# New source order at both ends of the FFN, with only TensorE held to the source from the output projection on

## The chip, the cores and the metric

The kernel runs on one core of one Trainium2 chip. Its time is what the device takes for one launch, in microseconds (us). Five engines work side by side, each through its own queue of instructions and in the order of that queue: TensorE (PE in the rows; PEld is its loading of weights), VectorE (DVE), ScalarE (ACT), GpSimd (POOL) and SyncE (SP), which issues nearly all transfers from memory. They wait for each other through semaphores.

## The reference, cut to what matters

One step of a one-layer encoder: two branches of attention, mixed into `m`, then an output projection, an FFN and a final norm. What the change touches is the last part:

```python
def _merge_ffn(h, ya, yb, ga, gb, w_out, norm_ffn, w_up, w_down):
    m = jax.nn.sigmoid(ga) * ya + jax.nn.sigmoid(gb) * yb
    h = h + jnp.einsum('btd,de->bte', m, w_out)
    u = jnp.einsum('btd,df->btf', _rmsnorm(h, norm_ffn), w_up)
    return h + jnp.einsum('btf,fd->btd', jnp.square(jax.nn.relu(u)), w_down)
...
    y_prompt = _rmsnorm(h_p[:, N_META:], norm_final)
    y_sample = _rmsnorm(h_s, norm_final)
```

The model width D is 1024, the FFN width 4096, and the kernel treats 544 tokens at once (512 of the prompt and 32 of the sample stream).

## The kernel before, in words

**Arithmetic.** All large products are made in a short float format with a correction: a matrix `a` is split into a high part (`split_hi`, a copy by ScalarE, line 121) and a low part (`split_lo`, a subtraction by VectorE, line 124), and a product is the sum of three matmuls, high by high, low by high and high by low (`mm`, line 118). So every weight that arrives from memory costs one ScalarE and one VectorE instruction before TensorE can use it, and so does every operand.

**Output projection.** The loop near line 1272 runs over the eight 128-row blocks of D in the order 0, 4, 1, 5, 2, 6, 3, 7 (`WO_ORDER`). For each it takes the split weights `wh`/`wl`, makes 48 matmuls into two parts of PSUM (288 and 256 tokens), adds the result to `xres` on VectorE (line 1283), and calls `operands(d)`. That function builds the operands of the FFN's up products out of two `xres` blocks: the tiles `ba`, `bb`, `b2`, and their splits `hh0` to `hh3` and `hl0` to `hl3`, of which number 3 is last, since it needs `xres3` and `xres7`.

**FFN up.** 16 steps, `up_pair(g)` for g = 0 to 15, each 256 columns of w_up. A step uses a scheme with seven products in place of eight: X with weights a11, V with s1, X again with s2, V with s4, X with s3, Y with a12, X with a22; each is 12 matmuls of 272 columns. Between the products ScalarE copies X or V out of PSUM (`fa`, `fb`, lines 1376, 1390, 1393, 1403, 1417), and the copy of the first X into `fa` must be done before the third product may add onto X. The weights of a step are made by `pair_prep(g)`, a generator: each `go(prep, n)` puts n more of its steps into the program (loads `wr1`, `wr2`; the sums `s31` and `s24` on VectorE, lines 297 to 308; then the splits, whose high parts are called `whi`, `s2h` and so on, their low parts `wlo`, `s2l`). It runs one step ahead. Two buffers of `whi`/`wlo` and three of raw weights are shared by all.

**FFN down.** The result of a step, squared, is split into `uh`/`ul`. The 16 steps form eight chunks: step 0, then pairs of steps, then steps 13 to 15. The down product of a chunk is eight calls `down(i)`, put between the products of the next chunk's first two steps, at the places n = 1, 3, 5, 6 of each. Its weights `dr` are loaded two calls ahead and split one call ahead (`dh`/`dl`). The last chunk's down product has no step left to lie between: it is the tail. There `last(d, a, b, ..)` does the eight blocks d for the first 288 tokens, then for the other 256; `last_evac` scales (`dt`, line 1523) and adds; `final_part` transposes finished blocks by TensorE into `ps_fin`, from which ScalarE takes squares (`fj`, line 1328) and VectorE writes `ytok` (line 1329); `final_norm` scales and stores.

**What sets the order.** Up to the output projection a scheduler places the instructions of all engines. From line 1205 on, `manual_schedule` holds TensorE, ScalarE and VectorE to the order of the source; the loads on SP go by the scheduler.

Of the kernel before, what the change touches and what calls it, by code (L numbers as in the profile page):

```python
# [15 lines left out]
P = 128  # L16
# [31 lines left out]
def tile_hybrid_step(  # L48
# [182 lines left out]
    def add_unit(key, parts):  # L231
        units.append((key, parts))

    def unit_prep(n):
        key, parts = units[n]
        raw = wpool.tile([P, KD, P], F32, tag="raw", name=f"wr_{n}", bufs=3)
        k = 0
        for src in parts:
            kk = src.shape[0] // P
            SP.dma_start(raw[:, k: k + kk, :], src.rearrange("(k p) n -> p k n", p=P))  # L240
            k += kk
        if parts[0].shape[0] == D and key[0] in IN_KEYS:
# [20 lines left out]
    def pair_prep(g):  # L263
# [45 lines left out]
        split(A, 1, ["s1"], s31[:, 1:2])  # L309
        yield  # L310
        if g == 0:
            for i, nm in enumerate(("s2", "s4")):
                split(one(nm), 0, [nm], s24[:, i: i + 1])
        else:
            B = t(wpool, "whi", bufs=2), t(wpool, "wlo", bufs=2)
            split(B, 0, ["s2", "s4"], s24)
# [862 lines left out]
    for d in range(KD):  # L1179
# [23 lines left out]


    ordered = ctx.enter_context(tc.manual_schedule(
        engines={mybir.EngineType.PE, mybir.EngineType.Activation, mybir.EngineType.DVE}))


    act_set = ACT.preload_act_table_set("natural_log_exp_and_others")
# [62 lines left out]
    for n, d in enumerate(WO_ORDER):  # L1272
        xr = tmp([TM], f"xres{d}")
        POOL.tensor_tensor(xr, xh[:, d, M0:].bitcast(F32), xl[:, d, M0:].bitcast(F32), ALU.add)
        wh, wl = use(("wo", d))
        if n == KD - 2:
            prep = pair_prep(0)
            go(prep, 3)
        if n == KD - 1:
            go(prep, 4)  # L1280

        def evac_o(ci, a, b, ps, xr=xr):
            DVE.tensor_tensor(xr[:, a:b], ps, xr[:, a:b], ALU.add)
# [81 lines left out]
    def up_pair(g):  # L1365
# [13 lines left out]
        if g == 0:  # L1379

            own, prep = prep, pair_prep(1)
            go(prep, 1)
            drain(own)
        else:
            drain(prep)
            prep = pair_prep(g + 1) if g < 15 else iter(())
            go(prep, 1)
        yield
        product(V, W["s1"], BM, True)
        ACT.activation(fb[:, 1, :], vv, AF.Copy)  # L1390
# [49 lines left out]

    def down(i):
        c, d = dn[i]
        if i + 1 < len(dn):
            go(dpreps[i + 1], 1)
        dstart(i + 2)
        wh, wl = downs.pop((c, d))
# [40 lines left out]
            DVE.reciprocal(r2[:, a:b], r2[:, a:b])  # L1487


    dstart(0)  # L1490
    dstart(1)
    for c in range(NCH):
        for jj, g in enumerate(CHUNKS[c]):
            for n, _ in enumerate(up_pair(g)):
                if c == 0 and n == 5:
                    go(dpreps[0], 1)
                if c > 0 and jj < 2 and n in (1, 3, 5, 6):
                    d = 4 * jj + (1, 3, 5, 6).index(n)
                    down(8 * (c - 1) + d)
                    if c == 1:  # L1500
                        square(d)
                    if c == 2 and d == 2:
                        norm2()
    while tail:
        tail.pop(0)()
    alloc_ytok()
# [1 line left out]

    c = NCH - 1

    def last(d, a, b, psf):
        wh, wl = downs[c, d]
        ps = psf(f"ps_dn{c}_{d}_{a}")
        K = 2 * len(CHUNKS[c])
        for k in range(K):
# [3 lines left out]
        return ps  # L1519

    def last_evac(d, a, b, ps):
        dt_ = fpool.tile([P, TM], F32, tag="dt", name=f"dt{c}_{d}_{a}", bufs=2)
# [5 lines left out]
    (a, b), T0, T1 = OC[0], range(3), range(3, NTT)  # L1528
    for d in range(KD):
        if d + 1 < KD:  # L1530
            go(dpreps[8 * c + d + 1], 1)
        dstart(8 * c + d + 2)
        ps = last(d, a, b, (psa, pss)[d % 2])
        if d == 4:
            final_part(0, T0)
        rest_a = last_evac(d, a, b, ps)
    a, b = OC[1]
    for d in range(KD):
        ps = last(d, a, b, (psa, pss)[d % 2])
        if d == 0:  # L1540
            final_part(1, T0)
        if d == 1:
# [4 lines left out]
        if d == 7:
            final_part(1, T1)
            final_early(3, NTT)
        rest = last_evac(d, a, b, ps)  # L1550
# [36 lines left out]
```

## Time and profile before

| | us |
|---|---|
| median of the runs (3) | 843.84 |
| the runs, lowest to highest | 840.65 to 845.9 |
| the profiled execution, its own time | 841.46 |
| its span, first to last instruction | 839.7 |
| TensorE busy within the span | 804.4 (96%) |
| VectorE busy | 585.3 (70%) |
| ScalarE busy | 366.2 (44%) |
| GpSimd busy | 123.3 (15%) |

Moments below are us from the start of that span. The output projection takes it from 392.8 to 444.05, the FFN's steps with the downs between them from 444.3 to 783.7, the tail the rest. Reading the profile: a line of an instruction gives its start, its duration, its engine and line, and in brackets how long the engine had been idle before it and whose instruction released it. Matmuls overlap: each is listed with 0.28 to 0.30 us, but the next starts 0.12 to 0.13 us later, and this distance is what one costs.

### The profile page before, as it was taken

Reading aid. Unit: us, or ns where it says so; the run is one execution under the profiler, and the core shown is the slowest. Engines: PE = TensorE matmul, PEld = TensorE weight load, DVE = VectorE, ACT = ScalarE, POOL = GpSimd, SP = SyncE. Lnnn points to the kernel's source line nnn. Section 1 sums busy time; section 2 is a strip of 40 time slices with the busy share of each in tenths; the row PEclk is TensorE's granted clock in tenths of the full one; section 3 lists DMA queues with packets and bytes.
Section 4 is the critical chain, followed back from the end, with each engine's and each line's share of the span. In section 5 each row is a group of like instructions: output and inputs, shape, how many; then the busy total and the mean of one; then the engine's idle time right before and its main releaser. Section 6 shows DMA issues by size and latency. Waiting matters only on the chain.

```text
span 839.7 us, 15161 instructions
## 1 busy us (share of the span) xinstructions
PE 804.4 (96%) x6093; PEld 772.6 (92%) x6093; DVE 585.3 (70%) x1139; ACT 366.2 (44%) x722; POOL 123.3 (15%) x132
## 2 busy tenths in 40 slices
PE   8998999999999999999997999999999999999995
PEld 6867898898999989999997999999999999999995
DVE  5856358798768554466667888776667777798764
ACT  5761454555446523232445673343433344333332
POOL 4305112221121493025000000000000000000000
PEclk8999999999999999999998999999999999999998
DMA  8513223422521132323123142323333333322402
GB/s 244 153 47 100 51 48 98 122 77 59 143 64 51 52 100 77 96 82 101 55 84 115 48 126 73 111 81 90 90 102 101 101 92 98 101 77 63 113 2 107
DMA packets 133813, 75.38 MB, mean 90 GB/s; under 512 B 15056, under 2 KB 129024, under 8 KB 133744
## 3 DMA queue, kind: packets, MB, share of 16 engines
q1 hardware_dynamic: 132704, 72.27, 30.4%
q0 software_dynamic: 1024, 2.14, 1.1%
q8 instruction: 48, 0.79, 0.4%
q14 instruction: 21, 0.17, 0.1%
q10 hardware_dynamic: 16, 0.00, 0.0%
HBM read 69.57 MB, written 4.83 MB: 89 GB/s over the span
## 4 chain that ended last, share of the span: by engine, by line
PE 72%; DVE 13%; ACT 5%; POOL 3%; issue 3%; DMA 3%; SPq 0%; ACTq 0%; POOLq 0%; DVEq 0%
PE ps_dn L118 22%; PE ps_x L118 11%; PE ps_v L118 6%; PE ps_gb L118 5%; PE ps_ga L118 5%; PE ps_fv L118 3%; PE ps_y L118 3%; PE ps_yb L118 2%; PE ps_ya L118 2%; PE ps_wo L118 2%; PE ps_fk L118 2%; DVE wl L124 2%; ACT wh L121 1%; DMA wr<-in_w_in_dram 1%; PE ps_s L118 1%
## 5 line engine op out<-in xcount | busy, mean ns | idle before, releaser
L118 PE MATMUL ps_dn<-uh,dl 128*128 128x288 f32 (+1 forms) x416 | 120.7, 290 | 0.0
L118 PE MATMUL ps_dn<-uh,dh 128*128 128x288 f32 (+1 forms) x416 | 119.7, 288 | 0.9 <-ACT uh L121 0.9
L118 PE MATMUL ps_dn<-ul,dh 128*128 128x288 f32 (+1 forms) x416 | 120.1, 289 | 0.2 <-DVE ul L124 0.2
L121 ACT ACTIVATE wh<-wr 128x1024 fp32r<-128x1024 f32 x46 | 48.5, 1055 | 87.9 <-PE ps_yb L118 24.3
L124 DVE TENSOR_TENSOR wl<-wr,wh 128x1024 fp32r<-128x1024 f32 x46 | 68.7, 1494 | 19.2 <-ACT wh L121 18.8
L118 PEld LDWEIGHTS ps_dn<-uh,dh 128*128 128x128 f32 x416 | 78.5, 189 | 1.1 <-ACT uh L121 1.1
L243 POOL TENSOR_TENSOR wr<-wr,gmix 128x1024 f32<-128x1024 f32 x30 | 58.0, 1937 | 143.2 <-DMA wr<-in_w_in_dram 104.5
L118 PEld LDWEIGHTS ps_dn<-uh,dl 128*128 128x128 f32 x416 | 78.3, 188 | 0.5 <-DVE dl L124 0.5
L118 PEld LDWEIGHTS ps_dn<-ul,dh 128*128 128x128 f32 x416 | 78.3, 188 | 0.5 <-DVE ul L124 0.5
L1468 DVE TENSOR_TENSOR acc<-ps_dn,acc 128x288 f32<-128x288 f32 x96 | 41.1, 438 | 30.4 <-PE ps_dn L118 30.4
L1307 POOL DMA_DIRECT2D gfin<-in_norm_final_dram x1 | 0.6, 607 | 374.1 <-DVE s3l L124 374.1
L118 PE MATMUL ps_x<-hh,whi 128*128 128x272 f32 x124 | 36.1, 291 | 1.5 <-ACT fa L1376 1.3
L124 DVE TENSOR_TENSOR dl<-dr,dh 128x512 fp32r<-128x512 f32 (+1 forms) x56 | 36.3, 648 | 1.7 <-ACT dh L121 1.6
L118 PE MATMUL ps_x<-hh,wlo 128*128 128x272 f32 x124 | 35.9, 290 | 0.5 <-DVE wlo L124 0.5
L118 PE MATMUL ps_v<-hl,whi 128*128 128x272 f32 x124 | 36.0, 290 | 0.0
L118 PE MATMUL ps_v<-hh,whi 128*128 128x272 f32 x124 | 35.8, 289 | 0.0
L118 PE MATMUL ps_x<-hl,whi 128*128 128x272 f32 x124 | 35.8, 289 | 0.0
L118 PE MATMUL ps_v<-hh,wlo 128*128 128x272 f32 x124 | 35.8, 288 | 0.0
L124 DVE TENSOR_TENSOR wlo<-s,whi 128x512 fp32r<-128x512 f32 (+1 forms) x31 | 29.4, 947 | 6.3 <-ACT whi L121 6.3
L935 ACT ACTIVATE sb<-sb,m 128x144 f32<-128x144 f32 (+3 forms) x32 | 18.3, 573 | 35.1 <-DVE m L930 35.1
L121 ACT ACTIVATE dh<-dr 128x512 fp32r<-128x512 f32 (+1 forms) x56 | 33.2, 593 | 0.0
L1403 ACT ACTIVATE x<-ps_x 128x272 f32<-128x272 f32 x16 | 6.4, 397 | 53.2 <-PE ps_x L118 53.1
(511 smaller groups left out, 2467.0 us busy)
## 6 DMA issues: line engine op xcount, KB each, us to landing
wr<-in_w_up_dram SPq DMA_DIRECT2D x62, 256.0 KB, 3.4
wr<-in_w_in_dram SPq DMA_DIRECT2D x30, 512.0 KB, 3.9
dr<-in_w_down_dram SPq DMA_DIRECT2D x48, 256.0 KB, 3.1
wr<-in_w_out_dram SPq DMA_DIRECT2D x8, 512.0 KB, 3.9
dr<-in_w_down_dram SPq DMA_DIRECT2D x8, 384.0 KB, 3.9
cb<-cPd SPq DMA_DIRECT2D x8, 264.0 KB, 4.1
x_t<-in_x_prompt_dram SPq DMA_DIRECT2D x4, 512.0 KB, 5.7
gvraw<-in_w_in_dram SPq DMA_DIRECT2D x4, 512.0 KB, 8.6
```

The source lines that it names most:

```text
L118: return TE.matmul(out, lhsT, rhs, start=start, stop=stop, skip_group_check=True)
L121: ACT.activation(out, in_, AF.Copy)
L124: (eng or DVE).tensor_tensor(out, in_, hi.bitcast(F32), ALU.subtract)
L243: POOL.tensor_tensor(raw, raw, gmix.unsqueeze(2).to_broadcast([P, KD, P]), ALU.mult)
L935: exps.append(ACT.activation(sb, sb, AF.Exp, bias=m, scale=-1.0, accum_out=rs).ins)
L1307: POOL.dma_start(late["gfin"], norm_final.partition_broadcast(P))
L1403: ACT.activation(x3, xv, AF.Copy)
L1468: DVE.tensor_tensor(acc[d][:, a:b], ps[:, :w], acc[d][:, a:b], ALU.add)
```

## The change

Apart from the order, nothing is computed differently; both programs have the same number of instructions on each engine. There are six edits:

- **Scheduler.** `manual_schedule` keeps TensorE alone; ScalarE and VectorE are ordered by the scheduler to the end of the program.
- **First step's weights.** The loads of `pair_prep(0)` are put into the source one output block earlier; of its steps, one comes at the third block from the end, two at the second and three at the last, where it was three and four; the rest is spread over the first three products of step 0. A last load of output weights is issued ahead of them (`unit_load`).
- **First downs.** For chunk 0 the table `EARLY` starts the eight calls `down` at n = 3 of step 1 (three in step 1, five in step 2), no longer at n = 1.
- **Norm.** `norm2`, two matmuls and four VectorE instructions, comes one chunk later.
- **Last chunk's weights.** They are prepared at n = 2 and 4 of step 15, no longer by `down`.
- **Tail.** The first two blocks start with the parts of the chunk that are long done (steps 13 and 14: `range(K - 2)`), and take those of step 15 only after both; weights are prepared three blocks ahead; the three tiles of `final_part(0, T0)` come one by one after d = 4, 5 and 6; the last block of the second half is cut in two, with `final_part(1, T1)` in the middle.

```diff
     ordered = ctx.enter_context(tc.manual_schedule(
-        engines={mybir.EngineType.PE, mybir.EngineType.Activation, mybir.EngineType.DVE}))
+        engines={mybir.EngineType.PE}))
...
+        if n == KD - 3:
+            unit_load(nxt[0])
+            prep = pair_prep(0)
+            go(prep, 1)
         if n == KD - 2:
-            prep = pair_prep(0)
+            go(prep, 2)
+        if n == KD - 1:
             go(prep, 3)
-        if n == KD - 1:
-            go(prep, 4)
...
             own, prep = prep, pair_prep(1)
             go(prep, 1)
-            drain(own)
+            go(own, 1)
...
         product(V, W["s1"], BM, True)
         ACT.activation(fb[:, 1, :], vv, AF.Copy)
+        if g == 0:
+            go(own, 1)
         yield
         product(X, W["s2"], BN, False)
         ACT.activation(fa[:, 1, :], xv, AF.Copy)
+        if g == 0:
+            drain(own)
...
-        if i + 1 < len(dn):
+        if i + 1 < 8 * (NCH - 1):
             go(dpreps[i + 1], 1)
...
+    REGULAR = [{1: (0,), 3: (1,), 5: (2,), 6: (3,)}, {1: (4,), 3: (5,), 5: (6,), 6: (7,)}]
+    EARLY = [{3: (0,), 5: (1,), 6: (2,)}, {1: (3,), 2: (4,), 3: (5,), 5: (6,), 6: (7,)}]
...
-                if c > 0 and jj < 2 and n in (1, 3, 5, 6):
-                    d = 4 * jj + (1, 3, 5, 6).index(n)
+                for d in (EARLY if c == 1 else REGULAR)[jj].get(n, ()) if 0 < c and jj < 2 else ():
                     down(8 * (c - 1) + d)
                     if c == 1:
                         square(d)
-                    if c == 2 and d == 2:
+                    if c == 3 and d == 2:
                         norm2()
+                if jj == 2 and n in (2, 4):
+                    go(dpreps[8 * c + n // 2 - 1], 1)
+                    dstart(8 * c + n // 2 + 1)
...
+    first = [last_ps(d, 0) for d in range(2)]
+    for d in range(2):
+        last(d, 0, first[d], range(K - 2))
+    prep_last(2)
     for d in range(KD):
...
+        if d < 2:
+            ps = first[d]
+            last(d, 0, ps, range(K - 2, K))
+        else:
+            ps = last_ps(d, 0)
+            last(d, 0, ps, range(K))
+        rest_a = last_evac(d, 0, ps)
+        prep_last(d + 3)
+        if 4 <= d < 7:
+            final_part(0, [d - 4])
     for d in range(KD):
-        ps = last(d, a, b, (psa, pss)[d % 2])
+        ps = last_ps(d, 1)
+        if d < KD - 1:
+            last(d, 1, ps, range(K))
+        else:
+            last(d, 1, ps, range(3))
+            final_part(1, T1)
+            last(d, 1, ps, range(3, K))
+            final_early(3, NTT)
```

The order of instructions shows at three places what the diff alone doesn't.

**VectorE, from the end of the output projection into step 0, before.** `xres7` is the sum of the last output block, from which the last operands are built (`bb3`, `b23`, `hl3`); `wlo_0`, `s2l_0`, `s4l_0`, `s3l_0` are low parts of the weights of step 0.

```order
L124 TENSOR_TENSOR hl3_4675<-ba3_5161,hh3_4671 128x544
L124 TENSOR_TENSOR wlo_0_5171<-wr1_0_5098,whi_0_5170 128x512
L124 TENSOR_TENSOR wlo_0_5171<-s31_0_5104,whi_0_5170 128x512
L124 TENSOR_TENSOR s2l_0_5177<-s24_0_5106,s2h_0_5176 128x512
L124 TENSOR_TENSOR s4l_0_5181<-s24_0_5106,s4h_0_5180 128x512
L124 TENSOR_TENSOR s3l_0_5185<-s31_0_5104,s3h_0_5184 128x512
L1283 TENSOR_TENSOR xres7_5168<-ps_wo7_0_5188,xres7_5168 128x288
L1283 TENSOR_TENSOR xres7_5168<-ps_wo7_1_5214,xres7_5168 128x256
L1253 SCALAR_TENSOR_TENSOR bb3_5162<-ba3_5161,b23_5240 128x272
L1254 TENSOR_TENSOR bb3_5162<-b23_5240,bb3_5162 128x272
L124 TENSOR_TENSOR hl3_4675<-bb3_5162,hh3_4671 128x544
```

The same place with the change; `dl0_0` is the low part of the first weights of the down product, whose transfer is `dr0_0`, and `s31_1` belongs to the weights of step 1.

```order
L1294 TENSOR_TENSOR xres7_5168<-ps_wo7_0_5180,xres7_5168 128x288
L124 TENSOR_TENSOR dl0_0_5389<-dr0_0_5253,dh0_0_5388 128x256
L124 TENSOR_TENSOR s4l_0_5289<-s24_0_5106,s4h_0_5288 128x512
L1294 TENSOR_TENSOR xres7_5168<-ps_wo7_1_5206,xres7_5168 128x256
L124 TENSOR_TENSOR s3l_0_5306<-s31_0_5104,s3h_0_5305 128x512
L124 TENSOR_TENSOR wlo_1_5347<-wr1_1_5281,whi_1_5346 128x512
L1261 SCALAR_TENSOR_TENSOR bb3_5162<-ba3_5161,b23_5232 128x272
L1262 TENSOR_TENSOR bb3_5162<-b23_5232,bb3_5162 128x272
L124 TENSOR_TENSOR hl3_4675<-b23_5232,hh3_4671 128x544
L1269 SCALAR_TENSOR_TENSOR ba3_5161<-bb3_5162,b23_5232 128x272
L304 TENSOR_TENSOR s31_1_5330<-wr1_1_5281,wr2a_1_5282 128x1024
L124 TENSOR_TENSOR hl3_4675<-bb3_5162,hh3_4671 128x544
```

The second half of `xres7` stood behind the low parts of all five weights, and stands behind two instructions now, of which one needs the transfer `dr0_0`; the `hl3` that is made of `bb3`, on which the third product waits, has `s31_1` ahead of it.

**ScalarE, same place, before.** `fa0` is the copy of the first X of step 0, on which the third product waits.

```order
L121 ACTIVATE hh3_4671<-ba3_5161 128x544
L121 ACTIVATE whi_0_5170<-wr1_0_5098 128x512
L121 ACTIVATE whi_0_5170<-s31_0_5104 128x512
L121 ACTIVATE s2h_0_5176<-s24_0_5106 128x512
L121 ACTIVATE s4h_0_5180<-s24_0_5106 128x512
L121 ACTIVATE s3h_0_5184<-s31_0_5104 128x512
L1252 ACTIVATE b23_5240<-xres7_5168,prmT_187 128x544
L121 ACTIVATE hh3_4671<-bb3_5162 128x544
L1376 ACTIVATE fa0_5267<-ps_x0_5269 128x272
```

And with the change:

```order
L121 ACTIVATE hh3_4671<-ba3_5161 128x544
L121 ACTIVATE dh0_0_5388<-dr0_0_5253 128x256
L121 ACTIVATE s4h_0_5288<-s24_0_5106 128x512
L121 ACTIVATE dh0_1_5494<-dr0_1_5255 128x256
L121 ACTIVATE s3h_0_5305<-s31_0_5104 128x512
L121 ACTIVATE whi_1_5346<-wr1_1_5281 128x512
L1260 ACTIVATE b23_5232<-xres7_5168,prmT_187 128x544
L1387 ACTIVATE fa0_5259<-ps_x0_5261 128x272
L121 ACTIVATE hh3_4671<-b23_5232 128x544
```

The splits of a11, s1 and s2 have moved away ahead of `hh3`, `fa0` no longer stands behind a split of `bb3`, and two splits of weights of the down product, `dh0_0` and `dh0_1`, stand in front of it.

**ScalarE at the start of step 15, before.** `whi7_0` is the high part of the first weights of the tail, which takes a buffer that TensorE must have left; `fa15` is the copy on which the third product of step 15 waits.

```order
L121 ACTIVATE uh14_8949<-fa14_8951 128x544
L1417 ACTIVATE fb14_8952<-ps_x14_8953 128x272
L121 ACTIVATE whi7_0_9202<-dr7_0_9144 128x768
L1376 ACTIVATE fa15_9242<-ps_x15_9244 128x272
L121 ACTIVATE uh14_8949<-fb14_8952 128x544
L121 ACTIVATE a22h_15_9261<-wr1_15_8974 128x512
```

With the change:

```order
L121 ACTIVATE uh14_8949<-fa14_8951 128x544
L1432 ACTIVATE fb14_8952<-ps_x14_8953 128x272
L121 ACTIVATE a22h_15_9257<-wr1_15_8974 128x512
L121 ACTIVATE uh14_8949<-fb14_8952 128x544
L1387 ACTIVATE fa15_9238<-ps_x15_9240 128x272
L1401 ACTIVATE fb15_9239<-ps_v15_9241 128x272
L121 ACTIVATE whi7_0_9287<-dr7_0_9144 128x768
```

`whi7_0` has moved behind the copies `fa15` and `fb15`.

## Rows read from the trace of the kernel before

**Rows 1.** The page: TensorE's busy time; its granted clock in 40 slices, in tenths.

```profile
PE 804.4 (96%) x6093; PEld 772.6 (92%) x6093; DVE 585.3 (70%) x1139; ACT 366.2 (44%) x722; POOL 123.3 (15%) x132
...
PEclk8999999999999999999998999999999999999998
```

**Rows 2.** Busy time by stretch: its length, PE, PEld, DVE, ACT, POOL, granted clock, DMA.

```profile
444.00:451.00 7.00, 3.62 (x26) 3.14 (x25) 5.46 (x11) 4.22 (x9) 0.00 (x0) 1.00 0.38 111
451.00:458.20 7.20, 6.33 (x28) 6.00 (x29) 6.17 (x11) 3.67 (x8) 0.00 (x0) 0.54 0.41 120
...
500.00:770.00 270.00, 269.45 (x2135) 268.91 (x2134) 207.07 (x360) 105.25 (x202) 0.00 (x0) 1.00 0.32 91
770.00:783.60 13.60, 12.34 (x99) 12.11 (x98) 10.17 (x20) 3.28 (x7) 0.61 (x1) 1.00 0.46 127
```

**Rows 3.** TensorE in time, output projection to step 3: start, duration, [idle before <- releaser].

```profile
400.07 1.08 PE L118 MATMUL ps_wo<-mh,wh 128*128 128x288 f32 x7
...
406.13 1.08 PE L118 MATMUL ps_wo<-mh,wh 128*128 128x288 f32 x7
...
444.31 0.39 PE L118 MATMUL ps_x<-hh,whi 128*128 128x272 f32 x1 [0.27 <-ACT whi L121]
...
450.98 0.40 PE L118 MATMUL ps_x<-hh,s2h 128*128 128x272 f32 x1 [2.67 <-ACT fa L1376]
...
454.81 0.43 PE L118 MATMUL ps_v<-hh,s4l 128*128 128x272 f32 x1
455.04 0.43 PE L118 MATMUL ps_v<-hl,s4h 128*128 128x272 f32 x1
...
462.34 0.29 PE L118 MATMUL ps_x<-hh,whi 128*128 128x272 f32 x1
462.47 0.29 PE L118 MATMUL ps_x<-hh,wlo 128*128 128x272 f32 x1
...
466.80 0.40 PE L118 MATMUL ps_dn<-uh,dh 128*128 128x288 f32 x1 [0.88 <-ACT uh L121]
...
497.75 0.29 PE L118 MATMUL ps_x<-hh,whi 128*128 128x272 f32 x1
```

**Rows 4.** VectorE in time, same stretch.

```profile
437.42 1.22 DVE L124 TENSOR_TENSOR wl<-wr,wh 128x1024 fp32r<-128x1024 f32 x1 [0.51 <-ACT wh L121]
438.57 1.22 DVE L297 TENSOR_TENSOR s<-wr,wr 128x1024 f32<-128x1024 f32 x1
...
447.43 0.78 DVE L1283 TENSOR_TENSOR xres<-ps_wo,xres 128x288 f32<-128x288 f32 x2
```

**Rows 5.** ScalarE in time, same stretch.

```profile
448.24 0.75 ACT L1252 ACTIVATE b<-xres,prmT 128x544 f32<-128x544 f32 x1 [1.90 <-DVE xres L1283]
```

**Rows 6.** DMA issues from 425 to 470: count, KB each, median us to landing.

```profile
dr<-in_w_down_dram SPq DMA_DIRECT2D x6, 128.0 KB, 3.0
```

**Rows 7.** TensorE in time, step 15 and tail.

```profile
776.02 0.40 PE L118 MATMUL ps_x<-hh,whi 128*128 128x272 f32 x1 [1.26 <-ACT fa L1376]
...
783.80 0.29 PE L118 MATMUL ps_dn<-uh,wlo 128*128 128x288 f32 x1
...
790.49 0.29 PE L118 MATMUL ps_dn<-uh,lh 128*128 128x288 f32 x1
...
802.63 0.40 PE L118 MATMUL ps_dn<-uh,ll 128*128 128x288 f32 x1 [1.01 <-DVE ll L124]
...
827.77 0.82 PE L1326 MATMUL ps_fin<-ident,xres 128*128 128x128 f32 x6
```

**Rows 8.** ScalarE and VectorE in time, step 15 and tail.

```profile
774.84 0.84 ACT L121 ACTIVATE whi<-dr 128x768 fp32r<-128x768 f32 x1 [5.76 <-PE ps_v L118]
...
798.97 1.87 DVE L1329 TENSOR_TENSOR ytok<-ps_fin,gfin 32x512 f32<-32x512 f32 x3 [1.53 <-ACT fj L1328]
...
830.18 0.42 DVE L1523 TENSOR_TENSOR dt<-ps_dn,r 128x256 f32<-128x256 f32 x1
```

**Rows 9.** TensorE's waits by releaser: us in total, times, longest.

```profile
PE ps_u L118 <- DVE states L663: 2.1, 2, 1.8
```

More of the change, by code (lines that the diff above doesn't have):

```diff
@@ L232, in add_unit, with unit_load @@
         units.append((key, parts))
-    def unit_prep(n):
-        key, parts = units[n]
-        raw = wpool.tile([P, KD, P], F32, tag="raw", name=f"wr_{n}", bufs=3)
+    loads = {}
+    def unit_load(n):
+        raw = loads[n] = wpool.tile([P, KD, P], F32, tag="raw", name=f"wr_{n}", bufs=3)
         k = 0
-        for src in parts:
+        for src in units[n][1]:
             kk = src.shape[0] // P
@@ L241, in unit_prep @@
             k += kk
+    def unit_prep(n):
+        key, parts = units[n]
+        if n not in loads:
+            unit_load(n)
+        raw = loads.pop(n)
         if parts[0].shape[0] == D and key[0] in IN_KEYS:
@@ L311, in pair_prep @@
         if g == 0:
-            for i, nm in enumerate(("s2", "s4")):
-                split(one(nm), 0, [nm], s24[:, i: i + 1])
+            split(one("s2"), 0, ["s2"], s24[:, 0:1])
+            yield
+            split(one("s4"), 0, ["s4"], s24[:, 1:2])
         else:
@@ L1509, in tile_hybrid_step, with last @@
     c = NCH - 1
-    def last(d, a, b, psf):
+    K = 2 * len(CHUNKS[c])
+    def last(d, ci, ps, ks):
+        a, b = OC[ci]
         wh, wl = downs[c, d]
-        ps = psf(f"ps_dn{c}_{d}_{a}")
-        K = 2 * len(CHUNKS[c])
-        for k in range(K):
+        for k in ks:
             uh, ul = u_tile(c, k)
@@ L1518, in last, with last_ps, last_evac @@
                 mm(ps[:, : b - a], w_[:, k, :], x_[:, a:b], k == 0 and m == 0, k == K - 1 and m == 2)
-        return ps
-    def last_evac(d, a, b, ps):
-        dt_ = fpool.tile([P, TM], F32, tag="dt", name=f"dt{c}_{d}_{a}", bufs=2)
+    def last_ps(d, ci):
+        return (psa, pss)[d % 2](f"ps_dn{c}_{d}_{ci}")
+    def last_evac(d, ci, ps):
+        a, b = OC[ci]
+        dt_ = fpool.tile([P, TM], F32, tag="dt", name=f"dt{c}_{d}_{ci}", bufs=2)
         DVE.tensor_tensor(dt_[:, : b - a], ps[:, : b - a], r2[:, a:b], ALU.mult)
@@ L1526, in last_evac, with prep_last @@
         return dt_, a
-    (a, b), T0, T1 = OC[0], range(3), range(3, NTT)
-    for d in range(KD):
-        if d + 1 < KD:
-            go(dpreps[8 * c + d + 1], 1)
-        dstart(8 * c + d + 2)
-        ps = last(d, a, b, (psa, pss)[d % 2])
[L1534 to L1537, printed above, removed]
-    for d in range(KD):
-        ps = last(d, a, b, (psa, pss)[d % 2])
+    def prep_last(d):
+        if d < KD:
+            go(dpreps[8 * c + d], 1)
+            dstart(8 * c + d + 2)
+    T0, T1 = range(3), range(3, NTT)
+    first = [last_ps(d, 0) for d in range(2)]
+    for d in range(2):
+        last(d, 0, first[d], range(K - 2))
+    prep_last(2)
+    for d in range(KD):
+        if d < 2:
[8 more added lines that the diff above has]
+            final_part(0, [d - 4])
+    for d in range(KD):
+        ps = last_ps(d, 1)
[6 more added lines that the diff above has]
+            final_early(3, NTT)
         if d == 0:
@@ L1546, in tile_hybrid_step @@
             final_part(0, T1)
[L1547 to L1550, printed above, removed]
+        rest = last_evac(d, 1, ps)
         if d == 2:
```

## The prediction

> **What bounds the kernel now.** I read the page's busy times and the clock by slice first: TensorE is busy for 96% of the span, and of the 40 slices only one in the middle, the 22nd (441 to 462), shows less than full clock apart from the first and last [rows 1]. So a gain must come out of the few places where TensorE stands still or runs slowly. The busy times by stretch say where these are: from 500 to 770 it stands for 0.55 us in all, while VectorE works 207 of 270 us and ScalarE 105 [rows 2]. Nothing is to be had there, but something can be lost. From 444 to 451 it stands for 3.4 of 7 us; from 451 to 458.2 the clock is at 0.54, near the lower of its two levels (1.2 of 2.4 GHz) [rows 2]. Then TensorE's instructions in time give each stall with its releaser, and those of the releasing engine show why it was late.
>
> **The head, before.** An output block without a stall takes 6.06 us (400.07 to 406.13); with that step block eight would end at 400.07 + 7 × 6.06 = 442.5, and step 0 starts at 444.31 [rows 3]. The difference, 1.8 us, is mostly blocks whose low weights were late: `wl` starts at 437.42 behind the operands of the block before [rows 4]. Step 0 then takes 18.0 us (444.31 to 462.34) for 84 matmuls, which at 0.13 us or just under (462.34 to 462.47; 12 of them take 1.51) need 10.6: 7.4 us are lost [rows 3]. Of these 2.7 are the wait for `fa`, which ScalarE did behind `b` and a split; `b` waited for `xres7`, which VectorE took up at 447.43, behind low parts of weights [rows 4, 5]. Some 28 matmuls after the stall come 0.23 us apart (454.81 to 455.04) where 0.126 is normal: about 2.8 us more [rows 3]. Steps 1 and 2 with eight downs take 35.4 us (462.34 to 497.75) for 264 matmuls, 33.2 at full speed: 2.2 us are lost, half of it in the 0.88 for `uh` and what follows [rows 3].
>
> **The change, part by part: the head.**
> - *Output blocks.* VectorE now takes `wl` ahead of the later operands, and the sums for step 0 lie in its pauses. Gain 1.8: X starts at 442.5, if the splits of a11 and s1 are done; by the moved loads they are, about 440.3 (load 3 us, as [rows 6], then 0.6 us each).
> - *Step 0's third product.* X and V run until 445.5. ScalarE reaches `fa0` only behind `dh0_0`, which waits for a transfer. Its load is queued on SP behind loads that need buffers of weights already split, so it leaves at about 440.2 and lands after 3.0 us or somewhat more [rows 6], say 443.4. After it come four splits of 0.5 to 0.6 us, then `b23`; that needs the second half of `xres7`, which VectorE takes after `dl0_0` and `s4l`, at 445.0. So `b23` at 445.6, `fa0` at 446.2, third product at 446.65: stall 1.15. It needs `hl3` of `bb3` for its last matmuls. VectorE does two sums and two other halves of operands before, and `s31_1`, which like `s` costs 1.22 [rows 4]; `hl3` is done about 450.2, so TensorE waits about 2.15 more. Lost: 3.3 instead of 7.4. Gain 4.1.
> - *Steps 1 and 2.* `EARLY` gives `uh` two products more before the first down needs it (3 us against a stall of 0.88), and the splits find their weights. I take all 2.2 us. VectorE has about 30 us of work in the 30 us from 460 on, so small stalls may come back: 0 to 3 us, and I take 1.
>
> Head: 1.8 + 4.1 + 2.2 − 1.0 = 7.1 us.
>
> **The middle.** The PE order is the old one apart from `norm2`, whose wait moves with it (nothing). The scheduler puts `s31` of a coming step, which waits for a load, ahead of evacuations on VectorE. I follow this step by step at the rows' durations and find each product's inputs 3 to 5 us early. Cost taken: 0; the other bound is a rival below.
>
> **The tail.**
> - *Step 15.* `whi7_0` waited for its buffer, and `fa15` behind it: ScalarE starts `whi` at 774.84, after 5.76 us of idling, and TensorE waits 1.26 to 776.02 [rows 7, 8]. Now `fa15` stands ahead of it. Gain 1.4 with the gap's edges.
> - *First two blocks.* Block 0 starts at 783.67, one matmul before 783.80; block 2 at 790.49; 36 matmuls of 0.133 us need 4.8, so 2.0 us are stalls (for `uh`, `ul`, `wlo`) [rows 7]. With the old parts of both blocks first there are 24 matmuls, 3.2 us, to cover the splits of step 15's result. Gain 2.0.
> - *`final_part(0, T0)`.* Three `ytok` of together 1.87 us stood in front of `ll` on VectorE, and TensorE waited 1.01 [rows 7, 8]. One tile at a time and weights three blocks ahead: gain 1.2 with the edges.
> - *The end.* Block 7's matmuls end at 827.77, but `dt` starts at 830.18, behind `ytok` of the tiles transposed just then [rows 7, 8]. With nine matmuls (1.06 us) behind the transposes this runs beside them: gain 1.0.
>
> Tail: 5.6 us. Its weights are loaded earlier, but three raw buffers hold them back as before; I find the last split done about 0.7 us before its block, so this cover is thin.
>
> **Sum.** 7.1 + 5.6 = 12.7 us, off the profiled execution's own 841.46: 828.8. That execution is 2.4 below the median of 843.84, so on the runs' level 831. I put the forecast between, at 830.
>
> **The clock.** The stall of 2.7 us was followed by the lower clock; the stretch of 770 to 783.6, with 1.26 in it, stayed at 1.00, and so did, in the slices, a wait of 1.8 us for `states` [rows 1 to 3, 7, 9]. The new stalls, 1.15 and 2.15 with 1.1 us of matmuls between, lie between these cases, nearer to 1.8; I take no fall. The Trainium skill ("TensorE: Matmul & The Clock Gate", section "A second HAM failure mode: psum-queue depth-cycling") says that frequent short idling between groups of matmuls can make the clock fall again and again. By that rule the time would be that of the second rival below. The row of 1.26 us speaks against it, and none here shows two pauses this close, so it keeps a chance.
>
> **The rivals.**
> - *The forecast* (826 to 833, chance 0.50).
> - *The clock falls again* at step 0. The price is the 2.8 us of before: about 833 (830 to 835). For it: same place, 3.3 us of standing within 4.5. Against it: each pause is below 2.7. Chance 0.22.
> - *Head-of-line waits eat the head.* `dh0_0` on ScalarE and `dl0_0` on VectorE wait for one transfer; if it lands 3 us later than I have it, everything behind moves, `fa0` among it; the stall is then 4 us, the clock falls too, and steps 1 and 2 keep theirs. Head gain 7.1 − 3 − 2.8 − 1 = 0.3: about 837 (834 to 840). For it: the loads are moved together, and SP's queue is in order. Against it: 3.0 us for six loads [rows 6]. Chance 0.13.
> - *Slower: a wait in each step.* On VectorE `s31` waits for its load, and behind it stands the evacuation that lets the next product start. Each of 12 steps (3 to 14) lasts about 23 us (497.75 to 776), and VectorE is free in a quarter of the time [rows 2]. From 1.1 us per step on, the gain of 12.7 is gone; from 1.8 on (12.7 + 8.4 = 21 us in 12) it is slower by over 1%. At 2 us: 830 + 24 = 854. Against it: slack of 3 to 5 us as I find it. Chance 0.07, of which 0.04 over the bound.
> - *It does little.* The scheduler's order brings its own small stalls wherever old ones go: 838 to 845. Chance 0.04.
> - *Better.* `dr0_0` lands before it is needed, and neither of the two new stalls comes: 7.1 + 3.3 + 1 + 5.6 = 17 us: 825. Chance 0.04.
>
> **How the numbers follow.** The likeliest is 830. The range from 825 to 837 takes in the better case's value, the forecast, the clock case and half of the third: 0.04 × 0.5 + 0.50 + 0.22 + 0.07 = 0.81. The bound of 1%, about what a measurement of this kernel can tell from none, lies at 835.4. Faster by more: 0.50 + 0.22 + 0.04, and 0.03 of the third: 0.79. Within: 0.10 of the third, 0.04, and 0.03 of the slower case: 0.17. Slower: 0.04.
>
> **What would show it.** Step 0's X near 442.5; its third product near 446.7 with a pause of about 1.2 for `fa0` and another, about 2, inside it for `hl3`; all clock slices in the middle at 9; step 3 near 490.6; 12 steps of the same length as before; in the tail no wait for `uh`, `ll` or `fa` and `dt` within 0.6 us of the last matmul. The forecast is wrong if the clock drops in the slice of step 0, if TensorE's list of waits has new entries with a dozen occurrences, or if the `lh`/`ll` splits of the last blocks wait for their loads.

## The result, and the profile after

The changed kernel takes 836.55 us (median of 7 runs, 830.93 to 836.91); the kernel before, run beside it, took 841.89 (839.69 to 845.9). The ratio is 0.9912, with a 95% interval from 0.9888 to 0.9937: about 5 to 9 us of gain. The profiled execution took 836.91, with a span of 835.1.

The page of the changed kernel, TensorE's busy time and its clock by slice, the lines that answer to [rows 1]:

```profile
PE 805.6 (96%) x6093; PEld 775.9 (93%) x6093; DVE 583.5 (70%) x1139; ACT 376.2 (45%) x722; POOL 123.4 (15%) x132
...
PEclk9997999999999999999998999999999999999998
```

Two things stand out. The 22nd slice (438 to 459) is still below full clock. And the fourth slice (63 to 84) has fallen too, in a part of the program that is the same in both kernels. The busy times by stretch of the changed kernel (length; PE, PEld, DVE, ACT, POOL busy; granted clock; DMA share; GB/s) show both, and how much was being moved just ahead of the first:

```profile
444.00:452.40 8.40, 5.56 (x46) 5.33 (x44) 5.59 (x12) 4.16 (x10) 0.00 (x0) 1.00 0.83 234
...
454.00:463.00 9.00, 7.93 (x41) 7.61 (x42) 6.97 (x13) 4.66 (x11) 0.00 (x0) 0.63 0.00 0
...
72.00:84.00 12.00, 10.98 (x75) 9.08 (x76) 6.47 (x21) 0.07 (x1) 4.06 (x4) 0.62 0.21 57
```

The same stretch of the profile of the kernel before:

```profile
72.00:84.00 12.00, 10.77 (x103) 9.36 (x104) 8.34 (x27) 1.11 (x2) 5.03 (x4) 1.00 0.21 57
```

So the output projection, which began at 392.77 before, begins at 396.74 here, 3.97 us later, before anything that the change moves. Moments must be compared from there. TensorE in time, changed kernel, the lines that answer to [rows 3, 7]:

```profile
396.74 1.08 PE L118 MATMUL ps_wo<-mh,wh 128*128 128x288 f32 x7
...
446.38 0.29 PE L118 MATMUL ps_x<-hh,whi 128*128 128x272 f32 x1
...
452.46 0.39 PE L118 MATMUL ps_x<-hh,s2h 128*128 128x272 f32 x1 [2.90 <-ACT fa L1387]
...
454.10 0.59 PE L118 MATMUL ps_x<-hh,s2h 128*128 128x272 f32 x1 [0.24 <-ACT hh L121]
...
455.89 0.60 PE L118 MATMUL ps_x<-hl,s2h 128*128 128x272 f32 x1 [0.97 <-DVE hl L124]
456.28 0.43 PE L118 MATMUL ps_v<-hh,s4h 128*128 128x272 f32 x1
456.51 0.43 PE L118 MATMUL ps_v<-hh,s4l 128*128 128x272 f32 x1
...
464.28 0.29 PE L118 MATMUL ps_x<-hh,whi 128*128 128x272 f32 x1
...
497.46 0.29 PE L118 MATMUL ps_x<-hh,whi 128*128 128x272 f32 x1
...
781.77 0.30 PE L118 MATMUL ps_dn<-uh,whi 128*128 128x288 f32 x1
...
786.56 0.29 PE L118 MATMUL ps_dn<-uh,lh 128*128 128x288 f32 x1
...
795.87 0.27 PE L1337 MATMUL ps_fin<-ident,xres 128*32 128x128 f32 x1 [1.68 <-DVE xres L1548]
```

X of step 0 comes 49.64 us after the projection's start (51.54 before). Step 0 is no shorter: 446.38 to 464.28 is 17.9 us, of which 2.9 are one wait for `fa0`, and the matmuls behind it come 0.23 us apart again. Steps 1 and 2 are shorter (464.28 to 497.46). The tail has a wait that was not there, 1.68 us for `xres`. ScalarE in time, same kernel, shows what `fa0` stood behind:

```profile
445.14 0.66 ACT L121 ACTIVATE hh<-ba 128x544 fp32r<-128x544 f32 x1 [0.95 <-DVE ba L1254]
449.07 0.42 ACT L121 ACTIVATE dh<-dr 128x256 fp32r<-128x256 f32 x1 [3.27 <-DMA dr<-in_w_down_dram]
...
452.01 0.40 ACT L1387 ACTIVATE fa<-ps_x 128x272 f32<-128x272 f32 x1
```

ScalarE stood for 3.27 us on the transfer of `dr0_0`, and `fa0`, whose X was complete at about 448, came 4 us later. SP's queue shows when that load left, and the busy times by stretch what was moved until it landed; the last line is the same load in the kernel before, which took 2.2 us:

```profile
440.02 5.16 SPq L283 DMA_DIRECT2D wr<-in_w_up_dram  x4
445.29 0.94 SPq L343 DMA_DIRECT2D dr<-in_w_down_dram  x2
```

```profile
445.29:449.04 3.75, 3.75 (x33) 3.75 (x32) 1.51 (x3) 0.51 (x1) 0.00 (x0) 1.00 0.95 268
```

```profile
442.89:445.11 2.22, 1.55 (x11) 1.13 (x9) 1.50 (x4) 2.03 (x4) 0.00 (x0) 1.00 0.28 80
```

VectorE shows the tail's wait, and one in step 0:

```profile
453.99 1.22 DVE L304 TENSOR_TENSOR s<-wr,wr2a 128x1024 f32<-128x1024 f32 x1
455.12 0.71 DVE L124 TENSOR_TENSOR hl<-bb,hh 128x544 fp32r<-128x544 f32 x1
...
794.39 0.96 DVE L124 TENSOR_TENSOR ll<-dr,lh 128x768 fp32r<-128x768 f32 x1 [2.42 <-ACT lh L121]
795.27 0.45 DVE L1548 TENSOR_TENSOR xres<-xres,dt 128x288 f32<-128x288 f32 x1
```

In the tail `ll`, low part of late weights, stands ahead of the sum `xres` of block 3, which needs no transfer, and the transposes wait for that sum.

**All profiles by stage.** Each column is the distance between starts of two of TensorE's matmuls (the last one: to the end of the span), so what happens ahead of the projection plays no part. "start" is the moment at which the projection begins.

| profile | start | projection | step 0 | steps 1, 2 | steps 3 to 14 | step 15 | tail | sum |
|---|---|---|---|---|---|---|---|---|
| before | 392.77 | 51.54 | 18.03 | 35.41 | 273.83 | 12.09 | 56.03 | 446.9 |
| b_again | 395.96 | 51.51 | 16.29 | 35.67 | 273.79 | 12.11 | 55.97 | 445.3 |
| changed | 396.74 | 49.64 | 17.90 | 33.18 | 273.74 | 10.57 | 53.33 | 438.4 |
| a_again | 397.25 | 49.64 | 18.37 | 33.20 | 273.75 | 10.57 | 53.02 | 438.5 |
| e1_dh_late | 395.72 | 49.64 | 11.36 | 33.20 | 273.73 | 10.57 | 51.78 | 430.3 |
| e2_sched_only | 392.17 | 49.68 | 12.53 | 33.39 | 273.74 | 10.57 | 55.02 | 434.9 |
| e2_again | 391.23 | 49.63 | 14.35 | 33.18 | 273.74 | 10.57 | 56.50 | 438.0 |
| e3_source_order | 396.53 | 51.51 | 14.85 | 36.43 | 273.79 | 10.57 | 52.42 | 439.6 |
| e4_dh_ll | 394.74 | 49.62 | 11.32 | 33.20 | 273.73 | 10.57 | 51.52 | 430.0 |
| e5_ll_only | 396.56 | 49.67 | 18.34 | 33.20 | 273.74 | 10.57 | 51.52 | 437.0 |
| e6_dr_pool | 397.28 | 49.62 | 13.29 | 33.18 | 273.73 | 10.57 | 52.73 | 433.1 |
| e7_no_early | 396.32 | 49.67 | 10.80 | 33.55 | 273.73 | 10.57 | 53.56 | 431.9 |
| e8_old_head | 389.69 | 49.64 | 14.46 | 33.23 | 273.73 | 10.57 | 51.48 | 433.1 |
| e9_old_head_dh | 396.25 | 49.66 | 10.86 | 33.53 | 273.75 | 10.57 | 51.58 | 430.0 |

From the projection on, the change gains 8.4 to 8.5 us against the profile that the prediction was made from, and 6.8 to 6.9 against a second one of the kernel before (b_again), whose clock was low for a shorter time in step 0 (3.4 us, not 6.8). The interval of the ratio, 5 to 9 us, holds both. That the first profiled execution of the changed kernel is only 4.6 us under that of before is the 3.97 us of the first stretch.

### The profile page after: what moved, and what is told of

It is laid out like the page before. It is cut to its first block, busy times and chain, and to the rows that moved or that the text cites. A ratio compares the mean times of both kernels' runs of the same rounds, so it can differ in the third digit from the quotient of the medians.

```text
span 835.1 us, 15216 instructions
## 1 busy us (share of the span) xinstructions
PE 805.6 (96%) x6093; PEld 775.9 (93%) x6093; DVE 583.5 (70%) x1139; ACT 376.2 (45%) x722; POOL 123.4 (15%) x132
## 4 chain that ended last, share of the span: by engine, by line
PE 74%; DVE 10%; DMA 6%; ACT 3%; POOL 3%; issue 2%; SPq 0%; ACTq 0%; POOLq 0%; DVEq 0%
PE ps_dn L118 22%; PE ps_x L118 11%; PE ps_v L118 6%; PE ps_gb L118 5%; PE ps_ga L118 5%; PE ps_fv L118 3%; PE ps_y L118 3%; PE ps_yb L118 3%; PE ps_ya L118 3%; PE ps_wo L118 2%; PE ps_fk L118 2%; DMA wr<-in_w_in_dram 2%; DVE wl L124 2%; PE ps_gq L118 1%; PE ps_s L118 1%
## 5 line engine op out<-in xcount | busy, mean ns | idle before, releaser
L121 ACT ACTIVATE whi<-s 128x512 fp32r<-128x512 f32 (+1 forms) x31 | 25.9, 835 | 15.9 <-PE ps_v L118 15.3
```

The source lines that it names most:

```text
L121: ACT.activation(out, in_, AF.Copy)
```

## The experiments

**a_again**: the changed kernel, unaltered, to learn what repeats.

> The changed kernel once more, unaltered. In its first profile the output projection began at 396.74 us, 3.97 later than before, although the instructions up to there are the same; TensorE's clock stood at 0.87 between 60 and 100 us. Theory A: this fall comes by chance from run to run and is no part of the change. Then the projection starts near 392.8 or near 396.7 from profile to profile, and the times of the runs fall into two groups some 4 to 6 us apart (near 831 and near 836.5), of both kernels alike. Theory B: the change itself brings it (where the program lies, when it starts). Then nearly all runs stay near 836.5, and those of the kernel before don't split. Steps from the projection on, measured from its start, should repeat within 0.3 us under both.

Six runs: median 834.88 us (830.67 to 837.55), ratio 0.9905 (0.9874 to 0.9935). The stages repeat to 0.3 us apart from step 0 (17.90, 18.37), and the projection starts late again. The times of both kernels spread over some 7 us, those of before from 838.86 to 845.8 in the same session, but two clean groups, as A had them, can't be made out.

**b_again** and **e2_again**: the kernel before, unaltered, and the run e2_sched_only (below) once more, since until then the low clock after the wait for `states` had been seen in nine profiles of new source and in none of old.

> The kernel before, unaltered, for its profile. So far the lower clock after the wait for states near 71 us is in 9 of 10 profiles with new source and in none of 2 with the old source. Theory A: it comes by chance in either kernel. Then it is likely to be seen here or in the run beside this one, and the projection begins at 394 to 398 us where it is, at 390 to 393 where it isn't. Theory B: the new source brings it on. Then both begin at 390 to 393. From the projection on: 446.7 to 447.2 us under both.

> The kernel of the run sched_only once more, for its profile (old source, scheduler edit). Theory A: the lower clock near 72 us in this or in the run beside it; theory B: in neither. From the projection on 434.5 to 436 us, more if the wait for fa0 is long enough to cost the clock in step 0.

b_again took 843.03 us (median of 8; ratio 0.9998, 0.9968 to 1.0029), e2_again 829.46 (median of 2). TensorE's wait for `states` (2.1 us in two parts, the longer 1.8) and its clock from 72 to 84 us in b_again:

```profile
PE ps_u L118 <- DVE states L663: 2.1, 2, 1.8
```

```profile
72.00:84.00 12.00, 10.98 (x76) 9.28 (x77) 6.78 (x22) 0.07 (x1) 4.39 (x4) 0.64 0.21 57
```

So the kernel before has the fall too, and its projection then starts at 395.96: the change isn't needed for it, against theory B. In all fourteen profiles TensorE waits 1.8 us for `states` near 71 us; in ten the clock of 72 to 84 us is 0.50 to 0.67 and the projection starts at 394.7 to 397.3, in four (before, e2_sched_only, e2_again, e8_old_head) it is 1.00 and the projection starts at 389.7 to 392.8. With the new source that is nine of ten, with the old one of four: theory A, chance alone, would have it equally frequent in both, and so few can't show that.

**e1_dh_late**: the changed kernel, with `dh0_0` and `dh0_1` ordered behind `fa0`.

```diff
-        ACT.activation(fa[:, 0, :], xv, AF.Copy)
+        fa_copy = ACT.activation(fa[:, 0, :], xv, AF.Copy)
+        if g == 0:
+            head.append(fa_copy.ins)
...
-        split_hi(hi, raw)
+        split = ACT.activation(hi, raw, AF.Copy)
+        if c == 0 and d < 2:
+            after(split.ins, head)
```

> The changed kernel with one order added: ScalarE takes the splits dh0_0 and dh0_1 only after fa0. Theory A: the third product of step 0 waited 2.9 us because fa0 stood behind dh0_0, which waited for the transfer dr0_0; the fall of the clock followed from that wait. Then the wait for fa0 is under 0.6 us, that for the last operands under 1, no lower clock near 455, and step 0 lasts 11 to 12.5 us in place of 17.9: 5 to 6.5 us less from the start of the projection to the end. Rival: the chain xres7, b23, hl3 sets the third product whatever stands beside it: step 0 then stays above 16 us and the time moves by less than 1.5 us.

828.36 us (median of 6), ratio 0.9835 (0.98 to 0.9871). ScalarE and TensorE in time, this run:

```profile
447.68 0.40 ACT L1389 ACTIVATE fa<-ps_x 128x272 f32<-128x272 f32 x1
447.98 0.65 ACT L121 ACTIVATE hh<-b 128x544 fp32r<-128x544 f32 x1
448.52 0.41 ACT L352 ACTIVATE dh<-dr 128x256 fp32r<-128x256 f32 x1
```

```profile
450.45 0.40 PE L118 MATMUL ps_x<-hl,s2h 128*128 128x272 f32 x1 [0.40 <-DVE hl L124]
```

`fa0` is copied 2.3 us after step 0's start, not 5.6; the only wait left in step 0 is 0.40 us, the clock stays at full, and step 0 takes 11.36 us. Theory A holds, and the rival falls. One order on ScalarE was worth 8.1 us from the projection on (438.4 to 430.3; 6.5 in step 0, the rest in a tail whose transfer came a little earlier).

**e2_sched_only**: the kernel before, with the scheduler edit and nothing else.

```diff
     ordered = ctx.enter_context(tc.manual_schedule(
-        engines={mybir.EngineType.PE, mybir.EngineType.Activation, mybir.EngineType.DVE}))
+        engines={mybir.EngineType.PE}))
```

> The kernel before with the scheduler edit alone (TensorE held to the source, ScalarE and VectorE by the scheduler). Theory A: the order of the output projection (wl ahead of later operands) gives 1.4 to 1.8 us by the edit alone, steps 1 and 2 keep their wait for uh (lose about 1 us), step 15 its gap or not as the scheduler puts whi7_0; step 0 has dh0_0 just ahead of fa0, so it waits for that transfer still: 2 to 5 us less than before in all, measured from the start of the projection. Rival: the scheduler's order is worth nothing without the new source order: within 1 us of before.

830.76 us (median of 6), ratio 0.9855 (0.9817 to 0.9893). From the projection on it takes 12.0 us less than the first profile of before and 3.5 less than the whole change. In e2_again, where the wait below was 1.47 and the clock fell after it, the two differences are 8.9 and 0.4 to 0.5. TensorE's wait in step 0, this run:

```profile
446.08 0.39 PE L118 MATMUL ps_x<-hh,s2h 128*128 128x272 f32 x1 [1.05 <-ACT fa L1376]
```

Both expectations miss: the edit alone gives the projection's 1.9 us, 5.5 in step 0 (3.7 in e2_again), the 2.0 of steps 1 and 2 (which the prediction had put down to `EARLY`, not in this kernel) and step 15's 1.5. In the tail it gives 1.0, or takes 0.5 in e2_again, where the clock fell again at 788.7, behind a wait of 2.05 us for `xres`.

**e3_source_order**: the changed kernel, with ScalarE and VectorE held to the new source order.

```diff
     ordered = ctx.enter_context(tc.manual_schedule(
-        engines={mybir.EngineType.PE}))
+        engines={mybir.EngineType.PE, mybir.EngineType.Activation, mybir.EngineType.DVE}))
```

> The changed kernel with the scheduler edit undone: ScalarE and VectorE in the new source order too. Theory A: in that order dh0_0 stands far behind fa0 and xres7 is taken as soon as it is there, so step 0 shows no wait for a transfer and no fall of the clock: 12 to 14 us in place of 17.9; the output projection gets its three late wl back (plus 1.2 to 1.8 us). In sum 2 to 4 us less than the changed kernel from the start of the projection on. Rival: the scheduler's order of the two engines carries most of the gain; then this kernel is slower than the changed one by 2 us or more.

836.1 us (median of 6), ratio 0.9926 (0.9896 to 0.9955): not to be told from the changed kernel in time, and by stage the sum of neither theory. The projection has its late `wl` back (51.51). Step 0, without any wait for a transfer, takes 14.85 us, with waits of 1.46 for `fa` and 1.15 for `fb`, which stand behind late operands in source order; steps 1 and 2 take 36.43, more than before, though `EARLY` is in. Step 15 is at 10.57: here the new source alone closes that gap, as the scheduler alone did in e2. So each half of the change gains about as much as the whole or more (446.9 to 434.9 or 438.0, and to 439.6), and the gains don't add.

**e4_dh_ll** and **e5_ll_only**: in the tail, low parts of late weights ordered behind the sum of the block that was just finished; e4 has the order of e1 as well.

```diff
-            DVE.tensor_tensor(hs[d][:, a:b], hs[d][:, a:b], dt_[:, : b - a], ALU.add)
+            sums.append(DVE.tensor_tensor(hs[d][:, a:b], hs[d][:, a:b], dt_[:, : b - a], ALU.add).ins)
...
-        split_lo(lo, raw, hi)
+        low = DVE.tensor_tensor(lo, raw, hi.bitcast(F32), ALU.subtract)
+        if final and sums:
+            after(low.ins, sums[-1:])
```

> The changed kernel with two orders added: ScalarE takes dh0_0 and dh0_1 after fa0 (as in the run dh_late), and in the tail VectorE takes the low part ll of weights for block d + 3 only after the sum xres of block d. Theory A: the wait of 1.3 to 1.7 us for xres in front of final_part(0, T0) comes from the scheduler's having put ll, which waits for a transfer, ahead of that sum. Then that wait is gone, the tail from its first matmul to the end of the span takes 51.5 to 52 us in every profile, and the whole span from the start of the output projection about 430 us. Rival: the transfer itself is what the tail waits for; then the wait moves to the matmuls of a later block and the tail stays near 53.

> The changed kernel with the order of the tail alone (ll after xres). Step 0 should stay at 17.5 to 18.5 us with the wait for fa0 of 2.9 to 3.5 and the lower clock. Theory A: tail 51.5 to 52 us in place of 53.0 to 53.3, the rest as in the changed kernel: 437 us from the start of the projection to the end, 1.3 less. Rival: no difference from the changed kernel in the tail.

e4: 827.51 us (median of 4), ratio 0.9815 (0.9789 to 0.9841). e5: 833.89, ratio 0.9874 (0.9835 to 0.9912). The tail takes 51.52 us in both, 1.5 to 1.8 less than in the changed kernel, and the transposes in e4 wait for nothing:

```profile
785.11 0.60 PE L1341 MATMUL ps_fin<-ident,xres 128*32 128x128 f32 x4
```

Theory A holds. e5 is also a third profile of step 0 with `dh0_0` in front: 18.34 us, a wait of 2.8 for `fa0`, and the lower clock.

**e6_dr_pool**: the order of the changed kernel, but the first two loads of down weights come through GpSimd's queue, early.

```diff
-        SP.dma_start(raw, w_down[0, r0: r0 + P * n, P * d: P * d + P].rearrange("(k p) n -> p k n", p=P))
+        (POOL if c == 0 and d < 2 else SP).dma_start(raw, w_down[0, r0: r0 + P * n, P * d: P * d + P].rearrange("(k p) n -> p k n", p=P))
```

> The changed kernel with the first two loads of the down weights (dr0_0, dr0_1) issued by GpSimd, ahead of time, in place of SP's queue; the order of ScalarE and VectorE is that of the changed kernel. Theory A: dh0_0 stands in front of fa0 as before but no longer waits, so the wait for fa0 falls from 2.9 to 3.5 us to under 0.8; hl3 still has s31_1 ahead of it, so a second wait of 0.8 to 2 us stays; no lower clock; step 0 takes 12 to 13.5 us. Rival: what precedes fa0 on ScalarE, or xres7, is late for another reason than the transfer: step 0 stays above 16 us.

828.95 us (median of 4), ratio 0.9835 (0.981 to 0.986). TensorE's waits in step 0, this run:

```profile
450.47 0.40 PE L118 MATMUL ps_x<-hh,s2h 128*128 128x272 f32 x1 [0.39 <-ACT fa L1387]
...
452.11 0.39 PE L118 MATMUL ps_x<-hh,s2h 128*128 128x272 f32 x1 [0.24 <-ACT hh L121]
...
453.93 0.39 PE L118 MATMUL ps_x<-hl,s2h 128*128 128x272 f32 x1 [1.31 <-DVE hl L124]
```

With the transfer there in time the same order of ScalarE costs 0.39 us, so the splits in front of `fa0` hold it up only when the transfer is late. But the late transfer alone doesn't do it either. In e2_sched_only `dh0_0` started 53.0 us after the projection's start, later than in the changed kernel (52.3), and TensorE waited only 1.05 us, for there `fa0` comes right behind it:

```profile
445.19 0.42 ACT L121 ACTIVATE dh<-dr 128x256 fp32r<-128x256 f32 x1 [0.83 <-DMA dr<-in_w_down_dram]
445.63 0.40 ACT L1376 ACTIVATE fa<-ps_x 128x272 f32<-128x272 f32 x1
```

In the changed kernel four splits and `b23` lie between the two (449.07 to 452.01). It is the transfer and the work behind it, together, that make the stall of 2.9 us. The wait for `hl3`, with `s31_1` ahead of it, stays, as expected: step 0 takes 13.29 us, with the clock at full.

**e7_no_early**: e1 with `EARLY` undone.

```diff
-                for d in (EARLY if c == 1 else REGULAR)[jj].get(n, ()) if 0 < c and jj < 2 else ():
+                for d in REGULAR[jj].get(n, ()) if 0 < c and jj < 2 else ():
```

> The kernel of the run dh_late with the table EARLY undone: the first downs at n = 1 of step 1 again. Theory A (as the prediction had it): the wait of 0.88 us for uh comes back and steps 1 and 2 take 34 to 35.4 us in place of 33.2. Rival: the scheduler's order of ScalarE already brings uh in time, and EARLY is worth nothing: 33.2 to 33.5 us, as in the run of the scheduler edit alone.

829.3 us (median of 4), ratio 0.9838 (0.9808 to 0.9867). Steps 1 and 2 take 33.55 us, and steps 0 to 2 together 44.35 (44.56 in e1). The rival holds: under the scheduler `EARLY` is worth nothing. (The whole is 1.6 us above e1, for the tail's wait for `xres`, 1.91 us here, isn't there in e1.)

**e8_old_head** and **e9_old_head_dh**: e5 with the source of the head as it was before; e9 has `dh0_0` and `dh0_1` behind `fa0` too.

```diff
-        if n == KD - 3:
-            unit_load(nxt[0])
-            prep = pair_prep(0)
-            go(prep, 1)
         if n == KD - 2:
-            go(prep, 2)
-        if n == KD - 1:
+            prep = pair_prep(0)
             go(prep, 3)
+        if n == KD - 1:
+            go(prep, 4)
...
-            go(own, 1)
+            drain(own)
...
-                for d in (EARLY if c == 1 else REGULAR)[jj].get(n, ()) if 0 < c and jj < 2 else ():
+                for d in REGULAR[jj].get(n, ()) if 0 < c and jj < 2 else ():
```

> The run ll_only with the head's source edits undone (output projection, spreading of step 0's weights, EARLY); the scheduler edit, the norm's place and the new tail stay. Theory A: the head's source edits cost time under the scheduler, since they leave it free to put dh0_0 ahead of s4h and of fa0 by three splits; without them step 0 takes 12 to 13 us as in the run of the scheduler edit alone (17.9 to 18.4 in the changed kernel), no lower clock near 455, steps 1 and 2 33.2 to 33.6, the tail 51.5: 431 to 432.5 us from the start of the projection to the end, some 6 less than the changed kernel. Rival: they carry part of the gain of the output projection or of steps 1 and 2; then X starts later than 50.5 us after the projection's start, or steps 1 and 2 take over 34 us.

> The run old_head with dh0_0 and dh0_1 behind fa0 as well. Theory A: step 0 takes 10.8 to 11.5 us, the sum from the projection's start is 429.5 to 430.5, as in the run dh_ll, which has all of the head's source edits: these are then worth nothing by themselves. Rival: with the old source the low parts for step 0 come later than fa0, and step 0 stays above 12 us.

e8: 827.16 us (median of 4), ratio 0.9805 (0.9779 to 0.9831); e9: 828.31, ratio 0.9813 (0.9779 to 0.9846). In e8 the projection, steps 1 and 2 and the tail are as fast without the head's source edits; step 0 is longer than expected, 14.46 us, because the wait for `fa0` is 1.65 (1.05 in e2) and the clock fell once after it. TensorE's wait and the clock by stretch, e8:

```profile
444.16 0.39 PE L118 MATMUL ps_x<-hh,s2h 128*128 128x272 f32 x1 [1.65 <-ACT fa L1385]
```

```profile
446.00:452.00 6.00, 5.90 (x35) 5.91 (x36) 4.95 (x10) 3.98 (x8) 0.00 (x0) 0.72 0.00 0
```

From the projection on it is 3.9 us below e5. Over all profiles with `dh0_0` where the scheduler puts it and its load on SP, step 0 takes 12.5 to 14.5 us with the old head (three) and 17.9 to 18.4 with the new one (three): under the scheduler the head's source edits cost 3.4 us or more. It isn't that the transfer comes later with the new source: `dh0_0` starts 53.0 to 53.6 us after the projection's start in the three old ones and 52.2 to 53.0 in the three new ones. In e9 step 0 takes 10.86 us and the sum is 430.0, as in e4: with the order mended they are worth nothing either way. e4, e8 and e9, which can't be told from each other in time, have the lowest ratios here, some 1% below the changed kernel; the intervals of e1, e6 and e7 overlap with theirs.

## Why the prediction was right or wrong

- **The time.** 836.55 lies within the range, at its upper end, 6.5 us above the likeliest value. Of 12.7 us forecast from the projection on, 8.4 to 8.5 came: step 0 missed 4.0 and the tail 1.5, steps 1 and 2 gave 1.0 more, the other stages 0.3. That the time lies inside all the same is in part luck. The fall of the clock near 72 us, which the prediction did not count, put the projection 3.97 us later than in the profile that 830 was worked out from; and the range reaches to 837 only for half of the third rival, whose losses in steps 1 and 2 did not come.
- **Output blocks** (1.8): 1.9. Right, and by the scheduler alone (e2, e8: 49.7 and 49.6; in source order, e3, 51.5).
- **Step 0** (4.1): 0.1 in the first profile, −0.3 in the second, both against 18.03 (−1.6 and −2.1 against b_again's 16.29). This is the step that failed, in one of its terms: the arrival of `dr0_0`. The mechanism was in the prediction: `fa0` behind `dh0_0`, and that behind the transfer. X came at 49.64 us from the start of the projection, 49.7 forecast. But `dr0_0` was taken to leave at 440.2 and land by 443.4, which is 47.4 and 50.6 us after the projection's start. It left at 48.55 (445.29 on the changed kernel's clock), right behind four larger loads, and was there 3.8 us later, at 52.3 (449.07). That is 1.7 us late, 1.1 by its leaving and 0.6 by its transfer. I had used the median of six loads, of which three took 2.2 to 2.4 us and three 3.5 to 3.8. The same load took 2.2 us in the kernel before, with 80 GB/s moved meanwhile, and 3.8 here with 268; with the scheduler edit alone (e2) it took 4.3. The stall grew by the same 1.7 us, to 2.9 for 1.15 (3.5 in a_again), and the clock fell with it: some 22 matmuls came 0.23 us apart in place of 0.126, about 2.3 us. That was the rival of the falling clock, with the cause named under head-of-line waits; each had been priced, at 0.22 and 0.13. e1 and e6 show it from both sides: move the split, or bring the load early, and the wait is 0 or 0.39.
- **The wait for `hl3`** (2.15): in the changed kernel the matmuls from 454.10 to 455.89 came about 1.9 late in all; in e6, without the lower clock, the waits are 1.31 for `hl` and 0.24 for `hh`. Right in place and nearly in size.
- **Steps 1 and 2** (2.2, less 1.0 for new stalls): 2.2. The size was right and the reason wrong. `EARLY` gives nothing (e2, e7, e8); the scheduler's order does. The 1.0 was not needed.
- **The middle** (0): 0.1 in twelve steps. The rival of a wait in each step falls.
- **Step 15** (1.4): 1.5. Right; either edit does it alone (e2, e3).
- **Tail.** First two blocks 2.0: 781.77 to 786.56 is 4.8 us, as forecast. The end 1.0: `dt` came about 0.5 us after the last matmul, for 2.4 before. `final_part(0, T0)`, 1.2: there it lost instead, for VectorE took `ll`, which waited for its weights, ahead of the sum that the transposes need (1.68 us). The prediction had called this cover thin, 0.7 us, but followed only `ll` to its own matmuls, not what stands behind it on VectorE. e4 and e5: with that order mended the tail gains 4.5, 4.2 forecast.
- **The clock.** I took 1.8 us for `states` as a wait that leaves the clock alone. That rested on one profile; in ten of fourteen the clock fell within 3 us of its end. In step 0 it fell with each wait for `fa0` of 2.7 to 3.5 us (five profiles), after 1.65 (e8) and 1.47 (e2_again), and stayed after 1.05 (e2) and in e3, whose waits were 1.46 and 1.15. In the tail it fell after 2.05 us for `xres` (e2_again) and stayed after 2.17 at the same place (e2). So from 1.5 to 2.2 us the length of a wait alone doesn't tell, in these profiles, whether the clock falls, and the one row of 1.26 us couldn't settle it. The rule of the Trainium skill that I weighed ("TensorE: Matmul & The Clock Gate", section "A second HAM failure mode: psum-queue depth-cycling"), that frequent short idling between groups of matmuls can make the clock fall again and again, is nearer to this than my reading of the one row, though no run here shows a clock that goes up and down in a loop.

## What to carry to other kernels

Letting a scheduler order two of three engines was worth as much by itself as the whole change or more (9 to 12 us against the first profile of before, 7 to 10 against the second). But here it put work that waits for a transfer (`dh0_0`, `ll`) ahead of work that needed none, and in a queue that runs in order all that follows waits too. Look in its order for each instruction released by a DMA, ask what the next ones hold up, and count the work between that instruction and the one that is waited for: with the same late transfer step 0 took 12.5 to 14.5 us with nothing between them, and 17.9 to 18.4 with five instructions. Two orders added by hand, of instructions that nobody was in a hurry for, then gave as much again (438.4 to 430.0). And price a load with what leaves ahead of it in its queue and with the traffic beside it, not with a median over loads that met less.

## What the runs showed of the hardware

A wait of 1.8 us in code that never changed was followed by the lower clock (0.50 to 0.67 over 72 to 84 us) in ten profiles of fourteen and not in four. From the end of that wait to the start of the projection it was 323.0 to 325.8 us in the ten and 318.8 to 319.8 in the four, so the fall goes with 3 to 7 us. Two kernels whose gain is about 1% can't be compared by one profile each from the beginning of the span. By distances between matmuls behind that place, most stages of one kernel repeat to 0.3 us; step 0 and the tail, where the clock can fall again, to 2. And one load of 128 KB that landed in 2.2 us while 80 GB/s were moved took 3.8 while 268 were; six profiles with `dr0_0` on SP and in front of `fa0` have 3.5 to 4.7.
